# Gate and up weights loaded four neighbouring rows to a partition, with the contraction in that order

## The chip, the cores and the metric

The kernel runs on one core of one Trainium2 chip. The metric is the device time of one execution in microseconds (us). The profiler took one further execution; all rows below are from that one.

## The reference

Two layers. In each, the residual stream `h` (1024 tokens by 1024 features, fp32) goes through an attention mixer and then through a mixture of experts:

```python
def hierarchical_moe(xn, w_group, w_router, w_gate, w_up, w_down):
    ...                       # router: 8 groups x 4 experts, the best group, two experts of it
    def expert_block(args):
        xb, e = args          # rows of one expert
        h = jax.nn.silu(xb @ w_gate[e]) * (xb @ w_up[e])
        return h @ w_down[e]
    ...                       # rows back to their tokens, weighted by the gates, summed
for l in range(DEPTH):
    h = h + hybrid_mixer(rms_norm(h, attn_norm[l]), ...)
    h = h + hierarchical_moe(rms_norm(h, ffn_norm[l]), ...)
return rms_norm(h, final_norm)
```

`w_gate` and `w_up` are [2, 32, 1024, 256] and `w_down` is [2, 32, 256, 1024], all fp32. So one expert has 1 MB each of gate, up and down weights, and one layer's 32 experts have 96 MB, each byte of it read once. A row of a gate or up matrix is 256 floats, 1 KB; a row of a down matrix is 4 KB.

## The kernel before

Every matmul of weights is done in three passes. A weight tile is split by ScalarE into a rounded part `hi` (L1468) and by VectorE into the rest `lo` (L1469), and the helper `mm3` (L195 to L197) multiplies high by high, high by low and low by high.

The experts are taken one after the other, each as one block of at most 96 rows. Per expert the stages are: a gather of its normed rows from DRAM (`xn_d`, written by `norm` in the router stage) by GpSimd's indirect DMA; eight transposes that put the features on the partitions (`flip_x`, L1479), split again into two parts (L185, L186); `gate_up`, 24 matmuls of 512 columns in which chunk k of the contraction multiplies features of chunk k with the gate and up columns of those features side by side; `silu` (L1493 on ScalarE, L1494); two transposes; `down`, 12 matmuls; and a scatter of the results by indirect DMA (L1517). Six pieces of 128 by 1024 weights are split per expert: four of gate and up, two of down. The order of the instructions of TensorE, ScalarE, VectorE and GpSimd is the order of the code; stages of neighbouring experts are interleaved there by hand.

SyncE's queue issues the weight loads. `load_gu` (L350, L351) loads an expert's gate and up weights in two halves `q`, four transfers of 512 KB; `load_dn` (L332) the down weights, one transfer of 1 MB. Gate and up tiles have room for the experts 0 to 4 before the first expert starts. From then on the loads of expert n + 5 are issued in the code where expert n begins, and each waits in SyncE's queue for its tile to come free. A partition of a half holds four rows that lie 128 rows apart in DRAM:

```python
ks = slice(q * 512, q * 512 + 512)
sp.dma_start(raw[q][:, :, 0:FF], wg_[ks].rearrange("(k p) n -> p k n", p=P))
sp.dma_start(raw[q][:, :, FF:], wu_[ks].rearrange("(k p) n -> p k n", p=P))
```

Ahead of the experts, the router stage works through eight tiles of 128 tokens: output projection, residual, `norm`, router. `norm` writes the normed tile with VectorE (L1103) and stores it (L1107). The last tile is done in two halves by GpSimd (`norm_half`, L1125). Expert 0's weights are split there too, with the `lo` parts on GpSimd (`halves`, L1113). The first gather (L1461) waits for the list of rows, at the end of a chain of small VectorE operations.

Of the kernel before, what the change touches and what calls it, by code (L numbers as in the profile page):

```python
# [82 lines left out]
def kernel(ctx: ExitStack, tc: tile.TileContext, x, positions, attn_norm, w_in, b_f, q_norm, w_uq,  # L83
# [48 lines left out]
    # gains, one feature per partition  # L132
# [31 lines left out]
    def rsqrt(dst, v, n, tag, c=1.0):  # L164
        """dst = c * v ** -0.5, with a Newton step behind the engine's own power."""
        y = small.tile([P, n], F32, name="rs_y", tag=f"rs_y{tag}")
        pool.tensor_tensor(y, v, mhalf[:, 0:n], op=OP.pow)  # L167
        t = small.tile([P, n], F32, name="rs_t", tag=f"rs_t{tag}")
        pool.tensor_tensor(t, y, y, op=OP.mult)  # L169
        pool.tensor_tensor(t, t, v, op=OP.mult)  # L170
        pool.tensor_scalar(t, t, -0.5 * c, 1.5 * c, op0=OP.mult, op1=OP.add)  # L171
        pool.tensor_tensor(dst, y, t, op=OP.mult)  # L172
# [9 lines left out]
    def split(hi, lo, src, scale=None):  # L182
        """hi + lo = src * scale, each with as many bits as one pass of the tensor engine carries."""
        if scale is None:
            act.activation(hi, src, AF.Copy)  # L185
            dve.tensor_tensor(lo, src, hi.bitcast(F32), op=OP.subtract)  # L186
        else:
            act.activation(hi, src, AF.Copy, scale=scale)
            dve.scalar_tensor_tensor(lo, src, scale, hi.bitcast(F32), op0=OP.mult, op1=OP.subtract)

    def mm3(ps, sh, sl, mh, ml, kcs, first=True, last=True):
        """ps += s.T @ m over the chunks, three passes."""
        n = len(kcs)
        for i, kc in enumerate(kcs):
            pe.matmul(ps, sh(kc), mh(kc), start=first and i == 0, stop=False)  # L195
            pe.matmul(ps, sh(kc), ml(kc), start=False, stop=False)  # L196
            pe.matmul(ps, sl(kc), mh(kc), start=False, stop=last and i == n - 1)  # L197
# [15 lines left out]
    # DRAM kept between phases  # L213
# [5 lines left out]
    def combined(l, i, ht, y_):  # L219
        """The residual stream's tile behind layer l - 1."""  # L220
        if l == 0:
            return ht
        for j in range(2):
            y = y_(j)
            sp.dma_start(y, y_d[l - 1][j * T + i * P:j * T + (i + 1) * P])
            dve.scalar_tensor_tensor(ht, y, gates[:, j, i:i + 1], ht, op0=OP.mult, op1=OP.add)  # L226
        if l < DEPTH:
            sp.dma_start(h_d[2 * l - 1][i], ht)
        return ht
# [106 lines left out]
    def gu_tiles(p, tags=("mix", "mix"), more=None):  # L336
        r = []
        for t in tags:
            q = p
            if t == "mix":  # L340
                gu_n[0] += 1
                if GUX and gu_n[0] > 8 and gu_n[0] % 9 == 0 and more is not None:
                    q, t = more, "gux"
            r.append(q.tile([P, 4, 2 * FF], F32, name="gu", tag=t))
        return r

    def load_gu(raw, wg_, wu_):
        for q in range(2):
            ks = slice(q * 512, q * 512 + 512)
            sp.dma_start(raw[q][:, :, 0:FF], wg_[ks].rearrange("(k p) n -> p k n", p=P))  # L350
            sp.dma_start(raw[q][:, :, FF:], wu_[ks].rearrange("(k p) n -> p k n", p=P))  # L351
# [6 lines left out]
    def mixer_open(l):  # L358
        """What a layer can load before the one in front of it is through."""
        # room of the latents, which takes tiles of the residual stream first  # L360
# [17 lines left out]
    def mixer(l, opened):  # L378
        h_in = [xv[i] for i in range(NT)] if l == 0 else h_d[2 * l - 1]
        h_out = h_d[2 * l]  # L380
        # operands of a forgetting head as rows: q_hi twice, q_lo, 1, 1, c_hi, c_lo; k_lo, k_hi, -c_hi, -c_lo, 1, 1
# [123 lines left out]
        # ---- values, queries and keys of the forgetting heads; beside it what hangs on misc -  # L505
# [32 lines left out]
        def forget_a():  # L538
            # log_sigmoid(z) = min(z, 0) - log1p(exp(-|z|)); log1p by its series in u / (2 + u)
            z, u, s1, s2 = t_("fz"), t_("fu"), t_("fs"), t_("fs2")  # L540
            fl.update(z=z, u=u, s1=s1, s2=s2)
            dve.tensor_tensor(z, misc[:, :, 0:H], bft[:, l][:, None, :].to_broadcast([P, NT, H]), op=OP.add)
            dve.scalar_tensor_tensor(u, z, -1.0, z, op0=OP.mult, op1=OP.min)
            act.activation(u, u, AF.Exp)
# [17 lines left out]
        def forget_c():  # L562
            # sums within a token tile, and behind them those of the tiles before
# [82 lines left out]
        def v_scale(g, tp):  # L646
            # a power of two that puts the largest value between 2**14 and 2**15
# [28 lines left out]
        def late_pools():  # L676
            # where the values and misc were: weights of the latent projections, tables of the rotation
# [256 lines left out]
        def fin_a(h):  # L934
            # normed rows: y / sqrt(mean(y * y) + eps * Z * Z), with y and Z scaled alike
# [24 lines left out]
        def fin_c(p, half, bank=1):  # L960
            ysb = pairs[p][0].rearrange("p t s d -> p t (s d)")
            # the bank of the second head's results, which the next pair comes to use later
# [10 lines left out]
        # the output projection's weights, two blocks of rows to a piece, where attention has done  # L973
# [120 lines left out]

        def norm(i):
            ht = hts[i]
            sp.dma_start(h_out[i], ht)
            if i < NT - 1:
# [4 lines left out]
                dve.scalar_tensor_tensor(xn, ht, rs[:, i:i + 1], gb, op0=OP.mult, op1=OP.mult)  # L1103
# [5 lines left out]
        def halves(j):  # L1109
            hi, lo = hl[j]  # L1110
            raw = early[0][j // 2][:, j % 2 * 2:j % 2 * 2 + 2].rearrange("p k n -> p (k n)")
            act.activation(hi, raw, AF.Copy)
            pool.tensor_tensor(lo, raw, hi.bitcast(F32), op=OP.subtract)  # L1113
# [3 lines left out]
        def norm_half(c):  # L1117
            """What the last tile's norm can do half by half."""
# [6 lines left out]
            pool.tensor_tensor(xn[:, cs], hts[NT - 1][:, cs], gb[:, cs], op=OP.mult)  # L1125
# [4 lines left out]
        # the router's operands are the tile before its norm: w_rt carries the gains, the gates' exponents the scales  # L1130
# [18 lines left out]
        def route_group(rg, a, b, lg=None):  # L1149
            """Experts, gates and ranks of the tokens of tiles a to b, and their entries in the blocks."""  # L1150
# [43 lines left out]
            # ranks within an expert by token; block NT holds the counts  # L1194
# [23 lines left out]
            # gates  # L1218
# [17 lines left out]
        # weights of the first experts, where attention's values and then its results have been  # L1236
        gu_n[0] = 0
        raw0 = v1.tile([P, 2, 4, 2 * FF], F32, name="V", tag="V")
# [11 lines left out]
        for i in range(NT):  # L1250
# [25 lines left out]
            if i == NT - 1:  # L1276
                # the first expert's gate and up weights in two parts, where those of w_o have been
# [35 lines left out]
        # rows of the blocks: which assignment sits where  # L1313
# [10 lines left out]
        # the experts' counts, and the number of further blocks they need  # L1324
# [7 lines left out]
        # behind the rows of the first experts  # L1332
# [13 lines left out]
    def more_tables(l):  # L1346
        """Blocks for the rows of an expert beyond the first RB: their experts, and which assignment sits where."""
# [28 lines left out]
        # of an assignment: the first further block of its expert, the block and the row its rank puts it in  # L1376
# [11 lines left out]
        # block of + qd - 1 where qd > 0, none elsewhere  # L1388
# [20 lines left out]
    def moe_open(l, v0, v1, mp, early, downs, dn_close, hl, hl_close, spare_close):  # L1409
# [16 lines left out]
        def expert(pools, wg_, wu_, wd_, gi, si, n=None):  # L1426
            """The stages of one block of rows, each to be issued where its engines have time."""
# [6 lines left out]
            def load_a():  # L1434
# [5 lines left out]
                e["raw"] = [raw[q][:, k:k + 2] for q in range(2) for k in (0, 2)]  # L1440
# [24 lines left out]
            def piece(j, eng=dve):  # L1465
                hi, lo = hl.popleft()
                raw = (e["raw"][j] if j < 4 else e["rawd"][j - 4]).rearrange("p k n -> p (k n)")
                act.activation(hi, raw, AF.Copy)  # L1468
                eng.tensor_tensor(lo, raw, hi.bitcast(F32), op=OP.subtract)  # L1469
                e["h"].append(hi)  # L1470
                e["l"].append(lo)
# [10 lines left out]
            def gate_up(q):  # L1482
                if q == 0:
                    e["gu"] = ps_([RB, 2 * FF], F32, name="gu")
                at = lambda w: lambda k: w[k // 2][:, (k % 2) * 512:(k % 2) * 512 + 512]
# [55 lines left out]
    def moe(l, m):  # L1541
# [16 lines left out]
        for n in range(NE + 1):  # L1558
# [19 lines left out]
            if l == DEPTH - 1 and n >= KEPT and len(kept) < NT:  # L1578
                # the weights are through: their room takes the residual stream for the last step
                for raw in gu_tiles(mp):  # L1580
                    for t in range(2):
                        kept.append(raw.rearrange("p k n -> p (k n)")[:, t * D:(t + 1) * D])
# [106 lines left out]
```

## Time and profile before

| What | Value |
|---|---|
| three runs | 1996.01, 1997.6 and 2002.56 us, median 1997.6 |
| profiled execution, first to last instruction | 1997.8 us |
| TensorE busy (matmul) | 1760.9 us, 88% |
| VectorE busy | 1347.5 us, 67% |
| ScalarE busy | 1187.7 us, 59% |
| GpSimd busy | 568.4 us, 28% |
| DMA | 427.11 MB, mean 214 GB/s |

No time of the profiled execution other than its span is given; the span lies 0.2 us over the median of the runs. The shares are means over stages that are limited by different things: attention, the router stage (about 490 to 634 us in layer 0 and 1466 to 1606 us in layer 1), the experts (about 634 to 966 us and 1606 to 1941 us) and the final norm. The expert stage has to be read by itself.

### The profile page before, as it was taken

How to read it: one execution, taken by the hardware profiler on the slowest of the kernel's cores; microseconds unless marked ns; L12 is line 12 of the kernel's file. 1: busy time of each engine (PE TensorE's matmuls, PEld its weight loads, DVE VectorE, ACT ScalarE, POOL GpSimd, SP SyncE). 2: the span in 40 equal slices, each digit the busy share in tenths (PEclk: the TensorE clock that was granted, in tenths of full speed). 3: DMA queues.
4: the chain of work that ended last, by engine and by line, in shares of the span. 5: the costliest groups of instructions: out<-in, count | busy, mean ns of one | idle time of the engine just before them, and what ended most of it. 6: DMA issues, size and time to landing. Idle time of an engine off the chain costs nothing. (4 is left out here: it accounts for less than half of the span.)

```text
span 1997.8 us, 33752 instructions
## 1 busy us (share of the span) xinstructions
PE 1760.9 (88%) x12509; PEld 1420.1 (71%) x12509; DVE 1347.5 (67%) x2172; ACT 1187.7 (59%) x2254; POOL 568.4 (28%) x857
## 2 busy tenths in 40 slices
PE   7999899999995999998499997999999689998870
PEld 6987688888883666666399786888888556666650
DVE  6454388887246888877555355888852678887756
ACT  4443278788214888877344235888841278887751
POOL 4001044234114333331230021623330333332305
PEclk9999999999997999999799998999999889999995
DMA  4257833553755999999742775334455499999986
GB/s 157 64 126 218 261 119 108 114 123 96 251 185 180 345 333 333 327 325 331 284 137 54 203 242 183 126 101 109 114 196 209 148 297 324 327 332 322 321 295 235
DMA packets 243684, 427.11 MB, mean 214 GB/s; under 512 B 22166, under 2 KB 168636, under 8 KB 240444
## 3 DMA queue, kind: packets, MB, share of 16 engines
q1 hardware_dynamic: 228092, 387.14, 61.2%
q0 software_dynamic: 14336, 33.58, 5.2%
q10 hardware_dynamic: 1088, 4.19, 0.7%
q8 instruction: 100, 1.64, 0.3%
q14 instruction: 68, 0.56, 0.1%
HBM read 347.24 MB, written 94.37 MB: 221 GB/s over the span
## 5 line engine op out<-in xcount | busy, mean ns | idle before, releaser
L1469 DVE TENSOR_TENSOR lo<-gu,hi 128x1024 fp32r<-128x1024 f32 x248 | 292.6, 1222 | 41.6 <-ACT hi L1468 41.6
L1468 ACT ACTIVATE hi<-gu 128x1024 fp32r<-128x1024 f32 x248 | 248.4, 1054 | 26.4 <-DMA gu<-in_w_up_dram 20.5
L195 PE MATMUL gu<-hi,V 128*96 128x512 f32 x512 | 214.8, 420 | 38.4 <-ACT V L185 38.4
L885 PE MATMUL S<-op 96*128 96x512 f32 (+3 forms) x960 | 228.8, 372 | 20.2 <-DMA op<-FK 13.2
L897 DVE TENSOR_REDUCE nm<-S 128x1 f32<-128x1024 f32 (+7 forms) x256 | 183.2, 752 | 69.3 <-PE S L889 69.3
L906 ACT ACTIVATE pr<-S,nm 128x1024 f32<-128x1024 f32 (+7 forms) x256 | 188.9, 754 | 38.0 <-DVE nm L897 37.9
L197 PE MATMUL gu<-hi,V 128*96 128x512 f32 x512 | 210.0, 410 | 0.0
L196 PE MATMUL gu<-lo,V 128*96 128x512 f32 x512 | 205.7, 402 | 0.0
L916 ACT ACTIVATE ph<-pt 128x512 f16<-128x512 f32 x288 | 157.1, 600 | 66.8 <-PE pt L914 65.8
L917 DVE SCALAR_TENSOR_TENSOR pl<-pt,ph 128x512 f16<-128x512 f32 x288 | 184.7, 682 | 8.6 <-ACT ph L916 7.8
L885 PEld LDWEIGHTS S<-op 96*128 96x128 f32 (+1 forms) x960 | 161.5, 196 | 37.5 <-DMA wor<-in_w_o_dram 14.5
L1517 POOL DMA_INDIRECT y<-V,sidx x64 | 59.7, 932 | 441.6 <-ACT V L1516 417.4
L914 PE MATMUL pt<-ident,pr 128*128 128x128 f32 x1152 | 154.9, 278 | 8.5 <-ACT pr L906 4.8
L1469 DVE TENSOR_TENSOR lo<-dn,hi 128x1024 fp32r<-128x1024 f32 x128 | 155.9, 1219 | 4.2 <-ACT hi L1468 3.9
L1468 ACT ACTIVATE hi<-dn 128x1024 fp32r<-128x1024 f32 x128 | 134.9, 1055 | 4.7 <-DMA dn<-in_w_down_dram 4.7
L195 PEld LDWEIGHTS gu<-hi,V 128*96 128x96 f32 x512 | 84.9, 166 | 74.1 <-ACT V L185 50.3
L914 PEld LDWEIGHTS pt<-ident,pr 128*128 128x128 f32 x1152 | 125.0, 143 | 13.7 <-ACT pr L906 12.9
L928 PE MATMUL y<-V,ph 128*128 128x64 f16 x2304 | 121.7, 193 | 2.8 <-ACT ph L916 1.6
L197 PEld LDWEIGHTS gu<-hi,V 128*96 128x96 f32 x512 | 84.6, 165 | 53.8 <-DVE V L186 21.9
L928 PEld LDWEIGHTS <-ph 128*128 128x128 f16 x2304 | 116.9, 98 | 5.2 <-ACT ph L916 1.8
L928 PE MATMUL y<-V,pl 128*128 128x64 f16 x1152 | 117.1, 193 | 1.1 <-DVE pl L917 1.0
L186 DVE TENSOR_TENSOR V<-pt,V 128x384 fp32r<-128x384 f32 x128 | 65.5, 552 | 69.1 <-ACT V L185 68.9
(363 smaller groups left out, 4318.5 us busy)
## 6 DMA issues: line engine op xcount, KB each, us to landing
gu<-in_w_gate_dram SPq DMA_DIRECT2D x124, 512.0 KB
gu<-in_w_up_dram SPq DMA_DIRECT2D x124, 512.0 KB
dn<-in_w_down_dram SPq DMA_DIRECT2D x60, 1024.0 KB
raw<-in_w_in_dram SPq DMA_DIRECT2D x48, 256.0 KB
h<-ht SPq DMA_DIRECT2D x17, 512.0 KB
FQ<-st SPq DMA_DIRECT2D x32, 256.0 KB
FK<-st SPq DMA_DIRECT2D x32, 256.0 KB
MQ<-st SPq DMA_DIRECT2D x16, 512.0 KB
```

Source lines behind the costliest of these rows:

```text
L195: pe.matmul(ps, sh(kc), mh(kc), start=first and i == 0, stop=False)
L196: pe.matmul(ps, sh(kc), ml(kc), start=False, stop=False)
L197: pe.matmul(ps, sl(kc), mh(kc), start=False, stop=last and i == n - 1)
L885: pe.matmul(o, a[0:k, qs], b[0:k, c0:c0 + n], start=bank not in started, stop=pi == len(passes) - 1 and not diag, skip_group_check=True)
L897: dve.tensor_reduce(nm, u["S"][:, col:col + (qb + 1) * P], axis=AX.X, op=OP.max, negate=True)
L906: act.activation(u["pr"][:, s], u["S"][:, s], AF.Exp, bias=nm, accum_out=zst[h // 2][:, qb, h % 2:h % 2 + 1])
L914: pe.transpose(pt[:, b], u["pr"][:, (4 * q + b) * P:(4 * q + b + 1) * P], ident)
L916: act.activation(u["ph"][:, ks], pt, AF.Copy, scale=P_SCALE)
L917: dve.scalar_tensor_tensor(u["pl"][:, ks], pt, P_SCALE, u["ph"][:, ks], op0=OP.mult, op1=OP.subtract)
L928: pe.matmul(yst[h][:, qb], a[:, b], v[:, kb, h % H, c], start=first_y[h], stop=(kb == qb and s == 2), skip_group_check=True)
L1468: act.activation(hi, raw, AF.Copy)
L1469: eng.tensor_tensor(lo, raw, hi.bitcast(F32), op=OP.subtract)
```

## The change

The rows of a gate or up matrix are spread over the partitions in another order. Partition p holds rows 8p to 8p + 7, rows 8p to 8p + 3 in half 0 and the other four in half 1, so that what a partition gets in one transfer is one run of 4 KB in DRAM where it was four runs of 1 KB. Gate and up lie in two separate blocks of a tile, where they lay side by side row by row.

Chunk k of the contraction now has the features 8p + k on its partitions. `norm` and `norm_half` write the normed rows with their columns in that order (column 128k + p holds feature 8p + k), so that the gather and the transposes stay as they were. To do so they read the residual tile and the gain eight floats apart. A matmul of `gate_up` reads its 512 moving columns as two runs of 256, and the pieces are split as two runs of 512. No instruction is added, removed or moved on any engine; only access patterns change.

```diff
@@ gu_tiles, load_gu
-            r.append(q.tile([P, 4, 2 * FF], F32, name="gu", tag=t))
+            r.append(q.tile([P, 2, 4, FF], F32, name="gu", tag=t))
...
-            ks = slice(q * 512, q * 512 + 512)
-            sp.dma_start(raw[q][:, :, 0:FF], wg_[ks].rearrange("(k p) n -> p k n", p=P))
-            sp.dma_start(raw[q][:, :, FF:], wu_[ks].rearrange("(k p) n -> p k n", p=P))
+            ks = slice(q * 4, q * 4 + 4)
+            sp.dma_start(raw[q][:, 0], wg_.rearrange("(p k) n -> p k n", k=KC)[:, ks])
+            sp.dma_start(raw[q][:, 1], wu_.rearrange("(p k) n -> p k n", k=KC)[:, ks])
@@ router stage
+        def by_chunk(t):
+            return t.rearrange("r (p k) -> r k p", k=KC)
+
+        def chunked(t):
+            return t.rearrange("r (k p) -> r k p", k=KC)
...
-                dve.scalar_tensor_tensor(xn, ht, rs[:, i:i + 1], gb, op0=OP.mult, op1=OP.mult)
+                dve.scalar_tensor_tensor(chunked(xn), by_chunk(ht), rs[:, i:i + 1], by_chunk(gb), op0=OP.mult, op1=OP.mult)
@@ halves
-            raw = early[0][j // 2][:, j % 2 * 2:j % 2 * 2 + 2].rearrange("p k n -> p (k n)")
+            raw = early[0][j // 2][:, :, j % 2 * 2:j % 2 * 2 + 2].rearrange("p g k n -> p g (k n)")
+            hi, lo = (w.rearrange("p (g n) -> p g n", g=2) for w in (hi, lo))
@@ norm_half
-            pool.tensor_tensor(xn[:, cs], hts[NT - 1][:, cs], gb[:, cs], op=OP.mult)
+            ps_ = slice(c * P // 2, c * P // 2 + P // 2)
+            pool.tensor_tensor(chunked(xn)[:, :, ps_], by_chunk(hts[NT - 1])[:, :, ps_], by_chunk(gb)[:, :, ps_], op=OP.mult)
@@ expert: load_a, piece, gate_up
-                e["raw"] = [raw[q][:, k:k + 2] for q in range(2) for k in (0, 2)]
+                e["raw"] = [raw[q][:, :, k:k + 2].rearrange("p g k n -> p g (k n)") for q in range(2) for k in (0, 2)]
...
-                raw = (e["raw"][j] if j < 4 else e["rawd"][j - 4]).rearrange("p k n -> p (k n)")
-                act.activation(hi, raw, AF.Copy)
-                eng.tensor_tensor(lo, raw, hi.bitcast(F32), op=OP.subtract)
+                raw = e["raw"][j] if j < 4 else e["rawd"][j - 4].rearrange("p k (g n) -> p (k g) n", g=2)
+                h_, l_ = (w.rearrange("p (g n) -> p g n", g=2) for w in (hi, lo))
+                act.activation(h_, raw, AF.Copy)
+                eng.tensor_tensor(l_, raw, h_.bitcast(F32), op=OP.subtract)
...
-                at = lambda w: lambda k: w[k // 2][:, (k % 2) * 512:(k % 2) * 512 + 512]
+                at = lambda w: lambda k: w[k // 2].rearrange("p (g k n) -> p g k n", g=2, k=2)[:, :, k % 2]
```

## Rows read from the trace of the kernel before

**Rows 1.** The page's part 2: the span in 40 equal slices, DMA share in tenths, GB/s

```profile
DMA  4257833553755999999742775334455499999986
GB/s 157 64 126 218 261 119 108 114 123 96 251 185 180 345 333 333 327 325 331 284 137 54 203 242 183 126 101 109 114 196 209 148 297 324 327 332 322 321 295 235
```

**Rows 2.** Busy us by stretch: stretch, length, five engines (x instructions), PEclk, DMA share, GB/s

```profile
740.00:850.00 110.00, 105.63 (x516) 73.13 (x515) 94.36 (x112) 91.24 (x134) 35.83 (x33) 1.00 1.02 329
867.00:956.00 89.00, 79.65 (x371) 54.66 (x370) 68.83 (x80) 64.90 (x96) 18.77 (x18) 0.96 1.02 333
1820.00:1930.00 110.00, 98.14 (x458) 67.53 (x457) 85.09 (x100) 80.53 (x117) 26.06 (x24) 0.95 1.02 335
```

**Rows 3.** Timeline of ScalarE: the silu of experts 2, 22, 31, then of 21, 31

```profile
658.90 0.36 ACT L1493 ACTIVATE hs<-gu 96x256 f32<-96x256 f32 x1
...
857.23 0.36 ACT L1493 ACTIVATE hs<-gu 96x256 f32<-96x256 f32 x1
...
955.63 0.38 ACT L1493 ACTIVATE hs<-gu 96x256 f32<-96x256 f32 x1 [1.51 <-PE gu L197]
...
1819.55 0.36 ACT L1493 ACTIVATE hs<-gu 96x256 f32<-96x256 f32 x1
...
1930.19 0.38 ACT L1493 ACTIVATE hs<-gu 96x256 f32<-96x256 f32 x1 [1.51 <-PE gu L197]
```

**Rows 4.** Waits, 860 to 956 us, then 1820 to 1930 us: total us, times, longest

```profile
PEld gu L195 <- ACT V L185: 11.4, 9, 3.6
ACT hi L1468 <- DMA gu<-in_w_up_dram: 10.0, 7, 3.6
...
ACT hi L1468 <- DMA gu<-in_w_up_dram: 10.4, 6, 4.0
```

**Rows 5.** Timeline of SyncE's queue: first gate load of experts 5 and 31, each layer

```profile
640.32 0.37 SPq L350 DMA_DIRECT2D gu<-in_w_gate_dram  x1
...
930.59 0.73 SPq L350 DMA_DIRECT2D gu<-in_w_gate_dram  x1
...
1612.05 0.37 SPq L350 DMA_DIRECT2D gu<-in_w_gate_dram  x1
...
1906.13 1.15 SPq L350 DMA_DIRECT2D gu<-in_w_gate_dram  x1
```

**Rows 6.** DMA view, 526 to 529 us (gate, up loads), then 1946 to 1949 us

```profile
DMA packets 1079, 1.07 MB, mean 357 GB/s; under 512 B 32, under 2 KB 1079, under 8 KB 1079
...
DMA packets 343, 1.24 MB, mean 412 GB/s; under 512 B 41, under 2 KB 41, under 8 KB 343
```

**Rows 7.** Two lines by themselves: duration in ns min/median/max, and the forms

```profile
L1178 DVE TENSOR_REDUCE ing<-tmp x6: 261/271/380, 562.8 to 1587.5; 128x8 f32<-128x64 f32 x4, 128x16 f32<-128x128 f32 x2
...
L1203 DVE TENSOR_REDUCE ee<-tmp x6: 286/286/421, 576.2 to 1592.2; 128x4 f32<-128x128 f32 x4, 128x8 f32<-128x256 f32 x2
```

**Rows 8.** Timeline of layer 0's last token tile, VectorE and GpSimd: start, us, what

```profile
595.87 1.28 DVE L1103 SCALAR_TENSOR_TENSOR xn<-ht,rs,gb 128x1024 f32<-128x1024 f32 x1
...
599.99 1.26 POOL L1125 TENSOR_TENSOR xn<-ht,gb 128x512 f32<-128x512 f32 x1 [5.75 <-DMA xn<-xn]
603.69 2.37 POOL L1113 TENSOR_TENSOR lo<-V,hi 128x1024 fp32r<-128x1024 f32 x1 [2.44 <-ACT hi L1112]
606.01 1.33 POOL L1125 TENSOR_TENSOR xn<-ht,gb 128x512 f32<-128x512 f32 x1
...
609.84 6.95 POOL L1113 TENSOR_TENSOR lo<-V,hi 128x1024 fp32r<-128x1024 f32 x3
...
610.01 2.21 DVE L1168 TENSOR_TENSOR eg<-eg,kg 128x16 f32<-128x16 f32 x1
...
616.85 0.17 DVE L1165 TENSOR_TENSOR e<-e,revg 128x8 f32<-128x8 f32 x1
...
624.33 1.26 POOL L1461 DMA_INDIRECT V<-xn,gidx  x1 [6.54 <-DVE gd L1221]
```

**Rows 9.** Matmuls by shape, 500 to 625 us, then the page's part 5

```profile
L1197 PE MATMUL rt<-OHs,onesb 128*128 128x256 bf16 x1 | 0.3, 270 | 0.0
...
L1197 PE MATMUL rt<-OHs,onesb 128*128 128x64 bf16 x1 | 0.2, 217 | 0.0
...
L195 PE MATMUL gu<-hi,V 128*96 128x512 f32 x512 | 214.8, 420 | 38.4 <-ACT V L185 38.4
```

More of the change, by code (lines that the diff above doesn't have):

```diff
@@ L1237, in mixer @@
         gu_n[0] = 0
-        raw0 = v1.tile([P, 2, 4, 2 * FF], F32, name="V", tag="V")
+        raw0 = v1.tile([P, 2, 2, 4, FF], F32, name="V", tag="V")
         early = [[raw0[:, 0], raw0[:, 1]]]
@@ L1581, in moe @@
                     for t in range(2):
-                        kept.append(raw.rearrange("p k n -> p (k n)")[:, t * D:(t + 1) * D])
+                        kept.append(raw[:, t].rearrange("p k n -> p (k n)"))
                         sp.dma_start(kept[-1], h_d[2 * l][len(kept) - 1])
```

## The prediction

> **What bounds the kernel now.** The change touches the expert stages and the norm in front of them, so I read those by themselves. I began with the slices of the page. The DMA share is at nine tenths in twelve of 40 slices, in two stretches, and these are the two expert stages [rows 1]. Full engines alone don't say that anyone waits for them, so the next view is the busy time by stretch [rows 2]. From 740 to 850 us TensorE's matmuls fill 105.63 of 110 us (0.96) at full granted clock, although the DMA share is 1.02 there. From 867 to 956 us they fill 79.65 of 89 (0.89), and from 1820 to 1930 us 98.14 of 110 (0.89), with the DMA engines as full as before. So TensorE sets the pace for most of a stage and something else does towards its end.
>
> The third view gives the size. There is one silu for each expert, and its start shows the rhythm [rows 3]. From expert 2 to expert 22 of layer 0 it is 857.23 - 658.90 = 198.33 us for 20 experts, 9.92 us each: TensorE's own pace. From expert 22 to expert 31 it is 98.40 us for 9 experts, where 89.25 would do: 9.15 us lost. In layer 1, expert 21 to expert 31 takes 1930.19 - 1819.55 = 110.64 us for 10 experts, against 99.17: 11.47 us lost. Together **20.6 us**, which is the most that faster weights can give back at this pace.
>
> The view of waits names the cause. In the late stretches ScalarE stands before the split of a gate and up piece until the load has landed, 10.0 us in layer 0 and 10.4 us in layer 1 [rows 4]. What TensorE's own row shows there, 11.4 us until ScalarE's split of the transposed rows, is the same delay one step on: that split stands in ScalarE's queue behind the piece that waits.
>
> Last, why late in the stage. Expert 5's first gate load is issued at 640.32 us and expert 31's at 930.59 us [rows 5]: 26 experts in 290.27 us, 11.16 us each, against TensorE's 9.92. The store of experts loaded ahead is used up by 1.2 us an expert until it is empty. Layer 1: 1906.13 - 1612.05 = 294.08 us, 11.31 us each.
>
> **The change part by part.**
>
> *The loads.* An expert's gate and up weights are 2.097 MB. Now they come as 2048 packets of 1 KB, afterwards as 512 of 4 KB. The trace has stretches with one size alone [rows 6]. With 1 KB packets, 1079 of them in 3 us, the engines move 357 GB/s; with 4 KB packets, 343 less the 41 small ones, 412 GB/s, both with the engines full. So the same bytes take 2.097 MB / 357 GB/s = 5.87 us now and 2.097 / 412 = 5.09 us then: 0.78 us less for each expert. Both stretches are undisturbed; in the expert stage the mean is 329 GB/s [rows 2], so everything takes longer there and the difference hardly less. Bounds: nothing below, if the engines give the expert stage some 330 GB/s whatever the packets are, and 0.78 x 357 / 329 = 0.85 us above. I take 0.78.
>
> How much is needed? To lose nothing, expert 31's loads would have to come 9.15 us earlier in layer 0 and 11.47 us in layer 1. Spread over 26 experts that is 0.35 us an expert (11.16 to 10.81) and 0.44 (11.31 to 10.87). 0.78 is well above both, so the store isn't empty before the end, TensorE keeps 9.92 us to the last expert and the gain is the whole 20.6 us. What lies above 0.44 buys nothing: with the loads at about 10.4 to 10.5 us, TensorE is the bound throughout.
>
> [...]
>
> *The loads at other places.* Five experts' weights come during the router stage, in the shadow of TensorE's projection. They get shorter by the same 0.78 us each and nobody waits for them in a row that I found; nothing.
>
> *The pieces and their matmuls.* The splits on ScalarE and VectorE read two runs of 512 where they read one of 1024. They have cover: in 110 us VectorE is busy 94.36 and ScalarE 91.24 [rows 2], so the 11 experts' 66 pieces could each cost 0.23 us more before VectorE is full. I take nothing. The 24 matmuls of an expert's gate_up have no such cover; there are 3 x 512 = 1536 in both layers [rows 9]. For a moving operand in several runs the nearest row is the count of ranks, L1197, which repeats runs of 32 columns: 217 ns for 2 runs and 270 ns for 8, and 192 more columns lie in that difference too. If the columns cost nothing, a run would cost at most 53 / 6 = 9 ns; if they account for it, nothing. I take nothing and keep 1536 x 9 ns = 13.6 us as the upper end.
>
> *The norm.* Its reads step eight floats. The nearest row is a reduction with a step of four floats, L1178: 261 ns for 64 elements, 380 for 128, 1.86 ns an element; a contiguous one, L1203, has 286 ns for 128 and 421 for 256, 1.05 ns [rows 7]. So a stepped element costs about 0.8 ns more. On VectorE's normed tile of 1024 that is 0.8 us, seven times a layer. These are hidden: of the last of them only the store matters, because GpSimd's first half of the last tile waits for it [rows 8]. That half starts at 599.99, takes 1.26 us, and GpSimd's next operation waits for ScalarE until 603.69 anyway; 2.4 us of cover.
>
> GpSimd's second half, at 606.01, is bare. Behind it in its queue stand the scale of the last tile and three subtractions (6.95 us from 609.84), and while these run VectorE's two-input operations stall (2.21 us for one of 128x16 elements, where one of 128x8 takes 0.17 behind them) [rows 8]. VectorE goes on freely at 616.85, and its chain ends in the first gather at 624.33, on which expert 0 waits. So a longer second half can shift the expert stage by as much. Price: 512 x 0.8 ns = 0.4 us a layer by VectorE's rows; bounds 0 (VectorE's chain gets ahead while GpSimd is late, and catches up) and a doubling, 1.33 us. I take 0.4 us, 0.8 us in both layers.
>
> [...]
>
> *Sum.* Against the profiled span of 1997.8 us: 1997.8 - 20.6 + 0.8 = **1978.0 us**. The span is 0.2 us above the median of the runs, 1997.6; I let that stand.
>
> **The rivals.**
>
> *Only a part comes back.* Loads gain less under contention than in the undisturbed stretches, or the indirect gathers and scatters, which share the engines, take some of it. For it: 329 GB/s in the stage against 357 with 1 KB packets alone, so packets aren't all that slows the loads. Against: the need is little more than half of 0.78. At half of the need, 0.2 us an expert, about half the loss stays: 1988 us.
>
> *No gain.* The stage is limited by what memory gives, not by packets, and the loads keep 11.2 us an expert. For it: the rate is between 321 and 345 GB/s in eleven of the twelve full slices [rows 1]. Against: stretches in rows 6 reach 412. The price is that of the norm alone: 1997.8 + 0.8 = 1998.6 us. [...]
>
> *Slower: the two runs cost TensorE time.* Every gate_up matmul pays a pause at the jump between the gate and the up run. TensorE is the bound for 20 of 32 experts already, so all of it would count, and slower experts need their loads later, so the 20.6 us come back anyway. It decides from (20.6 - 0.8) / 1536 = 13 ns a matmul; at 25 ns it is 38.4 us: 1978.0 + 38.4 = 2016 us. Against: at most 9 ns by rows 9.
>
> **How the numbers follow.** Whole gain 0.70, with its own range 1974 to 1983 us (the norm between 0 and 2.7 us, some of the loss left, a little more gained where the last experts run quicker than 9.92). A part, 1983 to 1991: 0.12. No gain, within 0.3% of 1997.6: 0.10. Slower: 0.08. A change within 0.3%, 6 us, can hardly be told from none here, as the runs before spread by 6.5 us. Faster by more than 0.3% (below 1991.6) is then 0.82, the same 0.10, slower 0.08. The range 1973 to 1990 us holds the whole gain and most of the second case.
>
> **What would show it.** Right: silus 9.92 us apart up to expert 31 in both layers; ScalarE's wait for gate and up loads near nothing in the late stretches; expert 31's first gate load some 10 us earlier after expert 5's; a DMA share that falls below 1 or a rate above 340 GB/s; L1103's successor near 2.1 us and L1125's near 1.7 us. Wrong: the same late gaps with 4 KB packets at 330 GB/s (second or third case), or gaps of over 10 us between silus from expert 2 on with TensorE's matmuls longer (fourth).

## The result

The changed kernel takes **1978.0 us** (median of 4 runs, 1977.16 to 1979.87) against 1996.8 us of the kernel before on the same chip (4 runs). The ratio is 0.9897, 95% interval 0.9878 to 0.9917: faster by about 1%, beyond the 0.3% within which the forecast could not tell a change from none. The profiled execution's span is 1978.1 us, against 1997.8. The device time of the changed kernel's profiled execution is 1979.87 us, 1.8 us above its span, and a device time lies as far above its span in the other kernels' runs. For the profiled execution of the kernel before only the span is on record, so its 1997.8 us is not to be compared with the medians directly.

The first view is the page's part 2 of the changed kernel, the answer to [rows 1].

```profile
DMA  4257732553754999998742775344456479999966
GB/s 158 65 130 218 258 125 100 113 128 79 274 181 156 335 367 366 360 353 307 246 141 54 205 239 189 125 104 108 108 186 226 156 259 358 362 360 357 345 217 219
```

The stretches of full DMA engines are still there, but they move some 360 GB/s where it was some 330, and they end earlier.

The busy time by stretch (columns as in [rows 2]) tells whether TensorE is held up at the end of a stage.

```profile
740.00:850.00 110.00, 105.61 (x515) 73.03 (x514) 94.25 (x112) 91.29 (x134) 35.82 (x33) 1.00 1.00 361
867.00:940.00 73.00, 69.85 (x342) 48.24 (x340) 62.13 (x73) 59.62 (x90) 18.26 (x18) 1.00 0.92 319
1800.00:1905.00 105.00, 100.61 (x489) 69.34 (x488) 89.57 (x107) 86.50 (x128) 28.84 (x27) 1.00 0.96 338
```

TensorE's share is now 0.96 in the late stretches too (69.85 of 73, 100.61 of 105), where it was 0.89, and its granted clock there is 1.00, where it was 0.96 and 0.95. The DMA share has fallen to 0.92 and 0.96 there, from 1.02: the loads are through before the stage is (in layer 0 the last transfer of expert 31's weights is issued at 914.63 us, and its silu comes at 946.19). The first stretch has the same busy times on VectorE and ScalarE as before (94.25 and 91.29 us, against 94.36 and 91.24), so splitting a piece as two runs costs neither of them anything that shows.

The rhythm, by the same silus as in [rows 3]: experts 2, 22 and 31 of layer 0, then 21 and 31 of layer 1.

```profile
658.81 0.36 ACT L1504 ACTIVATE hs<-gu 96x256 f32<-96x256 f32 x1
...
857.19 0.36 ACT L1504 ACTIVATE hs<-gu 96x256 f32<-96x256 f32 x1
...
946.19 0.38 ACT L1504 ACTIVATE hs<-gu 96x256 f32<-96x256 f32 x1 [1.51 <-PE gu L197]
...
1809.69 0.37 ACT L1504 ACTIVATE hs<-gu 96x256 f32<-96x256 f32 x1
...
1908.62 0.38 ACT L1504 ACTIVATE hs<-gu 96x256 f32<-96x256 f32 x1 [1.51 <-PE gu L197]
```

Experts 22 to 31 take 89.00 us where they took 98.40, and 21 to 31 of layer 1 take 98.93 where they took 110.64: 9.4 and 11.7 us, 21.1 us together. The waits from 860 to 956 us hold no row of ScalarE waiting for a gate or up load any more. What is left of the answer to [rows 4] is 0.58 us an expert for the transposed rows, as in the stretch from 740 to 850 us, where there is no wait for a gate or up load either (6.4 us for 11 experts):

```profile
PEld gu L195 <- ACT V L185: 5.2, 9, 0.6
```

SyncE's queue, first gate load of experts 5 and 31 of each layer, answers to [rows 5].

```profile
641.00 0.33 SPq L351 DMA_DIRECT2D gu<-in_w_gate_dram  x1
...
905.57 0.33 SPq L351 DMA_DIRECT2D gu<-in_w_gate_dram  x1
...
1603.13 0.34 SPq L351 DMA_DIRECT2D gu<-in_w_gate_dram  x1
...
1869.56 0.33 SPq L351 DMA_DIRECT2D gu<-in_w_gate_dram  x1
```

From expert 5 to expert 31 it is 264.6 us in layer 0 and 266.4 in layer 1, 25.7 and 27.7 us less than before, where the forecast looked for some 10. Only 9.4 and 11.7 of it come out of the stage; the rest is margin.

The norm of layer 0, answering to [rows 8]: the lines of VectorE and GpSimd by themselves (duration in ns min/median/max), then GpSimd's second half, its three subtractions, VectorE's first operation that is slow beside them (2.23 us, where the shortest of that line takes 0.17), and the first gather.

```profile
L1111 DVE SCALAR_TENSOR_TENSOR xn<-ht,rs,gb x14: 2081/2396/2418, 513.7 to 1558.8; 128x1024 f32<-128x1024 f32 x14
...
L1135 POOL TENSOR_TENSOR xn<-ht,gb x4: 2046/2068/2094, 601.4 to 1569.0; 128x512 f32<-128x512 f32 x4
```

```profile
606.37 2.09 POOL L1135 TENSOR_TENSOR xn<-ht,gb 128x512 f32<-128x512 f32 x1
...
610.89 6.95 POOL L1122 TENSOR_TENSOR lo<-V,hi 128x1024 fp32r<-128x1024 f32 x3
611.06 2.23 DVE L1178 TENSOR_TENSOR eg<-eg,kg 128x16 f32<-128x16 f32 x1
...
625.40 1.26 POOL L1471 DMA_INDIRECT V<-xn,gidx  x1 [6.54 <-DVE gd L1231]
```

Both operations are slower than before by more than was forecast, and the chain shifts as described: the three subtractions start 1.05 us later, and the first gather 1.07 us later. Not all of that is the norm's. The start of the scale of the last tile but one (L176 on GpSimd), which lies ahead of the last tile's halves, already comes 0.35 us later than before, and counted from it the gather is 0.72 us late. The first silu of the layer isn't late at all. Before, then changed:

```profile
592.31 0.19 POOL L176 TENSOR_SCALAR rs_v<-ss 128x1 f32<-128x1 f32 x1 [13.06 <-ACT xn L1101]
...
641.70 0.38 ACT L1493 ACTIVATE hs<-gu 96x256 f32<-96x256 f32 x1 [1.94 <-PE gu L197]
```

```profile
592.66 0.19 POOL L176 TENSOR_SCALAR rs_v<-ss 128x1 f32<-128x1 f32 x1 [14.62 <-ACT xn L1109]
...
641.61 0.38 ACT L1504 ACTIVATE hs<-gu 96x256 f32<-96x256 f32 x1 [1.15 <-PE gu L197]
```

The ledger of the two profiled spans: up to expert 31's silu of layer 0, 955.63 - 946.19 = 9.4 us gained; from there to expert 31's silu of layer 1, 974.6 - 962.4 = 12.1 us; from there to the end, 67.6 against 69.5, 1.9 us lost. The sum is 19.7 us before rounding (9.44 + 12.13 - 1.87), which is the difference of the spans.

### The profile page after: what moved, and what is told of

The parts are those of the page before. It is cut to its first block, busy times and chain, and to the rows that moved or that the text cites. A ratio compares the mean times of both kernels' runs of the same rounds, so it can differ in the third digit from the quotient of the medians.

```text
span 1978.1 us, 33744 instructions
## 1 busy us (share of the span) xinstructions
PE 1754.6 (89%) x12509; PEld 1414.8 (72%) x12509; DVE 1361.8 (69%) x2172; ACT 1188.2 (60%) x2254; POOL 568.7 (29%) x857
## 5 line engine op out<-in xcount | busy, mean ns | idle before, releaser
L1480 DVE TENSOR_TENSOR lo<-gu,hi 128x1024 fp32r<-128x1024 f32 x248 | 292.5, 1221 | 18.8 <-ACT hi L1479 18.8
L1479 ACT ACTIVATE hi<-gu 128x1024 fp32r<-128x1024 f32 x248 | 248.2, 1054 | 0.0
L195 PE MATMUL gu<-hi,V 128*96 128x512 f32 x512 | 210.9, 412 | 24.4 <-ACT V L185 24.4
L197 PE MATMUL gu<-hi,V 128*96 128x512 f32 x512 | 207.0, 404 | 0.0
```

What stands on the lines that cost most here:

```text
L1479: act.activation(h_, raw, AF.Copy)
L1480: eng.tensor_tensor(l_, raw, h_.bitcast(F32), op=OP.subtract)
```

## The experiments

All kernels ran beside the kernel before. In the first group of four its median was 1997.8 us (17 runs), in the second group of three 1997.5 us (23 runs).

**The size of the packets by itself.** All of the change's tiles, splits and two-run matmuls stay, but the partitions hold the old rows 128 apart, and the norm writes in the old order.

```diff
-            sp.dma_start(raw[q][:, 0], wg_.rearrange("(p k) n -> p k n", k=KC)[:, ks])
-            sp.dma_start(raw[q][:, 1], wu_.rearrange("(p k) n -> p k n", k=KC)[:, ks])
+            sp.dma_start(raw[q][:, 0], wg_.rearrange("(k p) n -> p k n", p=P)[:, ks])
+            sp.dma_start(raw[q][:, 1], wu_.rearrange("(k p) n -> p k n", p=P)[:, ks])
...
-                dve.scalar_tensor_tensor(chunked(xn), by_chunk(ht), rs[:, i:i + 1], by_chunk(gb), op0=OP.mult, op1=OP.mult)
+                dve.scalar_tensor_tensor(xn, ht, rs[:, i:i + 1], gb, op0=OP.mult, op1=OP.mult)
...
```

> The change's tiles, splits and matmuls (two blocks, two runs), with the rows of before: four runs of 1 KB, 128 rows apart, and the norm of before; the output is the reference's. If the packet's size is what gave the time: no gain, 1995 to 1999 us, silus late from expert 22 on, packets of 1 KB at about 330 GB/s in the expert stage. If it was the tile's layout (each transfer fills one run of 4 KB of a partition): 1978 us. If the two-run matmuls cost 9 ns each they show here as up to 13 us on top.

Measured: 1998.5 us (12 runs), ratio 1.0001, interval 0.9986 to 1.0017. The whole gain is gone. Its profiled execution was the longest of the twelve (span 2009.3 us), but the picture in it is that of the kernel before; here the late stretches, with TensorE at 63.77 of 73 (0.87) and 94.59 of 110 (0.86):

```profile
867.00:940.00 73.00, 63.77 (x291) 43.61 (x290) 55.55 (x65) 51.89 (x76) 16.47 (x16) 0.95 1.02 321
...
1820.00:1930.00 110.00, 94.59 (x426) 64.34 (x425) 80.37 (x94) 77.09 (x113) 24.09 (x23) 0.94 1.02 322
```

So the gain is in what one packet holds, not in the tiles' layout. Whether it is fewer packets or longer runs of neighbouring bytes in DRAM that helps, no kernel of the study separates. And as this kernel keeps the two-run matmuls and is no slower than before (1998.5 us against 1997.8), these cost nothing that can be measured: the rival that rested on them is out.

**Packets of half the size.** Two neighbouring rows to a partition, packets of 2 KB, and the norm in the order that belongs to them (a step of two floats). The eight transposes of an expert take their chunks in the sequence that goes with it.

```diff
-            sp.dma_start(raw[q][:, 0], wg_.rearrange("(p k) n -> p k n", k=KC)[:, ks])
-            sp.dma_start(raw[q][:, 1], wu_.rearrange("(p k) n -> p k n", k=KC)[:, ks])
+            rows = lambda w: w[q * 512:q * 512 + 512].rearrange("(a p t) n -> p a t n", a=2, t=2)
+            sp.dma_start(raw[q][:, 0].rearrange("p (a t) n -> p a t n", t=2), rows(wg_))
+            sp.dma_start(raw[q][:, 1].rearrange("p (a t) n -> p a t n", t=2), rows(wu_))
...
-            return t.rearrange("r (p k) -> r k p", k=KC)
+            return t.rearrange("r (j t) -> r t j", t=2)
...
-                        k = 4 * q + c
+                        k = c % 2 * 4 + 2 * q + c // 2
```

> Two neighbouring rows to a partition and run, 2 KB packets; the norm steps two floats in place of eight; the output is the reference's. From the packet cost that the two sizes of the prediction imply (5.87 us for 1 KB, 5.09 for 4 KB, the same overhead for each packet), 2 KB should take about 5.35 us, 0.52 us less an expert, over the 0.35 and 0.44 that are needed: the whole gain, 1976 to 1979 us, no late silu in layer 0 and at most a trace of one in layer 1. If the gain goes with the load time instead, two thirds of it: 1984 us.

Measured: 1977.3 us (6 runs), ratio 0.9893, interval 0.9873 to 0.9914. The whole gain again. The DMA view of 740 to 850 us, where the engines are full, for the changed kernel, then for 2 KB and for 1 KB (the kernel of the experiment above):

```profile
DMA packets 11580, 39.72 MB, mean 361 GB/s; under 512 B 1900, under 2 KB 1900, under 8 KB 11572
```

```profile
DMA packets 16612, 38.75 MB, mean 352 GB/s; under 512 B 1877, under 2 KB 1877, under 8 KB 16604
```

```profile
DMA packets 25145, 36.02 MB, mean 327 GB/s; under 512 B 1790, under 2 KB 21229, under 8 KB 25137
```

The rate rises with the packet: 327, 352, 361 GB/s. These are rates of everything in the stretch; the down weights come in 4 KB rows in all three kernels. The time does not follow the rate. At 2 KB the loads of experts 5 to 31 take 10.49 us each in layer 0 and 10.53 in layer 1 (273.7 us for 26), below the 10.81 and 10.87 that the forecast called the need, and nothing is lost. With both packets the store of experts lasts to the end, and the faster loads of 4 KB bought nothing more (1978.0 us, against 1977.3 with 2 KB); the other outcome that was written down, 1984 us in proportion to the load time, is out. At which pace between those of 1 KB and 2 KB packets the loss ends, no run shows.

**Each side's own pace.** To see what the loads do when TensorE doesn't hold them up, the third pass of gate_up is left out (8 of 24 matmuls an expert), once in the changed kernel and once in the kernel before.

```diff
-            pe.matmul(ps, sh(kc), ml(kc), start=False, stop=False)
-            pe.matmul(ps, sl(kc), mh(kc), start=False, stop=last and i == n - 1)
+            pe.matmul(ps, sh(kc), ml(kc), start=False, stop=not low and last and i == n - 1)
+            if low:
+                pe.matmul(ps, sl(kc), mh(kc), start=False, stop=last and i == n - 1)
...
-                    range(4 * q, 4 * q + 4), first=q == 0, last=q == 1)
+                    range(4 * q, 4 * q + 4), first=q == 0, last=q == 1, low=False)
```

> The changed kernel without the third pass of gate_up (16 of 24 matmuls an expert; the low part of the rows is left out), so that TensorE needs about 8.2 us an expert and the loads bound the late part of the stage: it shows the loads' own pace with 4 KB packets. Theory by the period measured in the changed kernel (a load is issued every 10.2 us with full engines): late silus 10.1 to 10.3 us apart. By the forecast's 0.78 us: 10.4 to 10.5 us. Rival (the period there was held up by TensorE, the loads could do much better): 9.6 us or less. The time about 1940 to 1965 us.

> The same cut in the kernel before: the third pass of gate_up left out, 1 KB packets. Theory (the loads bound it): late silus 11.2 to 11.3 us apart, from an earlier expert on than in the kernel before, and the end of a layer's experts hardly earlier, 0 to 4 us a layer: 1989 to 1998 us. The difference to the same cut with 4 KB packets prices the packets with TensorE out of the way: 0.78 us for each expert over 26 experts and two layers would be 41 us, 1.0 us would be 52 us. Rival (TensorE's pace set it, packets don't matter): both cuts take the same time, 70 us or more below the kernel before.

Measured: 1962.2 us with 4 KB packets (4 runs, 1957.0 to 1964.8), ratio 0.9819 to the kernel before, interval 0.9794 to 0.9844. With 1 KB packets 2002.1 us (10 runs, 1993.3 to 2009.0), ratio 1.0023, interval 1.0008 to 1.0038. The silus of experts 12 and 29 of layer 0, then of layer 1, first with 4 KB:

```profile
747.09 0.36 ACT L1505 ACTIVATE hs<-gu 96x256 f32<-96x256 f32 x1
922.03 0.36 ACT L1505 ACTIVATE hs<-gu 96x256 f32<-96x256 f32 x1
...
1698.97 0.36 ACT L1505 ACTIVATE hs<-gu 96x256 f32<-96x256 f32 x1
...
1875.19 0.37 ACT L1505 ACTIVATE hs<-gu 96x256 f32<-96x256 f32 x1
```

And with 1 KB:

```profile
747.86 0.36 ACT L1494 ACTIVATE hs<-gu 96x256 f32<-96x256 f32 x1
...
937.64 0.37 ACT L1494 ACTIVATE hs<-gu 96x256 f32<-96x256 f32 x1
...
1715.87 0.37 ACT L1494 ACTIVATE hs<-gu 96x256 f32<-96x256 f32 x1
...
1905.89 0.36 ACT L1494 ACTIVATE hs<-gu 96x256 f32<-96x256 f32 x1
```

Seventeen experts take 174.94 and 176.22 us with 4 KB, 10.29 and 10.37 us each; with 1 KB 189.78 and 190.02 us, 11.16 and 11.18 each. These are the loads' own paces: in the early part, where loads are still ahead, the silus of both kernels are 8.7 us apart, and here ScalarE waits for the down weights, which are loaded through the same queue. The waits from 740 to 850 us, with 4 KB, then with 1 KB:

```profile
ACT hi L1480 <- DMA dn<-in_w_down_dram: 17.4, 10, 2.2
```

```profile
ACT hi L1469 <- DMA dn<-in_w_down_dram: 21.4, 10, 2.7
```

TensorE's 9.92 us with all three passes lies under both paces. The difference is 0.81 to 0.87 us an expert. From the first silu to the last of each layer the same two executions differ by 19.3 and 20.1 us, 0.76 us over 2 x 26 experts, and the medians differ by 39.9 us, 0.77. The profiled execution with 1 KB is the fastest of its ten, 8.8 us under their median, so the true difference may be somewhat larger.

The pair also says which engine bounds each kernel. The same third of gate_up's matmuls is worth some 16 us where packets are 4 KB (1978.0 to 1962.2, from two groups of runs) and nothing where they are 1 KB (2002.1 us, against 1997.5). With 1 KB the kernel even came out 4.7 us slower than the kernel before, outside the 1989 to 1998 us that were expected; why is open.

**The norm put back in order.** The changed kernel with the norm of the kernel before.

```diff
-                dve.scalar_tensor_tensor(chunked(xn), by_chunk(ht), rs[:, i:i + 1], by_chunk(gb), op0=OP.mult, op1=OP.mult)
+                dve.scalar_tensor_tensor(xn, ht, rs[:, i:i + 1], gb, op0=OP.mult, op1=OP.mult)
...
-            pool.tensor_tensor(chunked(xn)[:, :, ps_], by_chunk(hts[NT - 1])[:, :, ps_], by_chunk(gb)[:, :, ps_], op=OP.mult)
+            pool.tensor_tensor(xn[:, cs], hts[NT - 1][:, cs], gb[:, cs], op=OP.mult)
```

> The change without its stepped norm reads: the normed rows are stored in feature order, so the experts multiply the wrong features (the output is wrong in that part, the work is the same). In the trace of the changed kernel the first gather of layer 0 starts 1.07 us later than before (625.40 against 624.33), yet the silu of expert 0 doesn't (641.61 against 641.70). If the norm's price is on the path, 1.0 us a layer comes back: some 1976 us. If it is absorbed between the gather and the first matmuls: 1978 us, and the silu of expert 0 is again within 0.2 us of where it was.

Measured: 1977.2 us (6 runs), ratio 0.9891, interval 0.9870 to 0.9911; 0.8 us under the changed kernel, less than the intervals can tell apart. The first silu of layer 0 is neither within 0.2 us of where it was nor 1 us earlier: it comes 2.4 us earlier than in the changed kernel, at 639.18 us. That isn't this norm's price, for L176 of the last tile but one is 2.7 us earlier already, and the kernel with the step in the transposes, its norm in order too, has its first silu at 641.63 us:

```profile
589.95 0.19 POOL L176 TENSOR_SCALAR rs_v<-ss 128x1 f32<-128x1 f32 x1 [13.07 <-ACT xn L1109]
...
639.18 0.38 ACT L1504 ACTIVATE hs<-gu 96x256 f32<-96x256 f32 x1 [1.92 <-PE gu L197]
```

So this run decides nothing on a price of 1 us.

**The norm by itself.** The opposite cut: the kernel before with the stepped norm alone, edited at the same two places in the other direction.

```diff
-                dve.scalar_tensor_tensor(xn, ht, rs[:, i:i + 1], gb, op0=OP.mult, op1=OP.mult)
+                dve.scalar_tensor_tensor(chunked(xn), by_chunk(ht), rs[:, i:i + 1], by_chunk(gb), op0=OP.mult, op1=OP.mult)
...
```

> The kernel before with the change's norm alone: the normed rows are stored with their columns in the new order, the weights and the contraction are left in the old one, so that normed features and weights don't belong together. Theory (the norm costs little and is absorbed): VectorE's normed tile about 2.40 us and GpSimd's half about 2.07 us, as in the changed kernel, against 1.28 and 1.30; the first gather of a layer 0 to 1.1 us later; the time 1997.8 + 0 to 2 us, no difference that can be measured. Rival (the gain of the whole change hides a real price of the norm, which late weights or the rise of the clock pay back in the changed kernel): the first silu of a layer comes 1 us or more later in both layers and the time is 2 to 4 us over the kernel before.

Measured: 1997.4 us (12 runs), ratio 0.9999, interval 0.9984 to 1.0014. The two lines have the prices that they have in the changed kernel, here with the mean of one in ns behind the busy us:

```profile
L1109 DVE SCALAR_TENSOR_TENSOR xn<-ht,rs,gb 128x1024 f32<-128x1024 f32 x14 | 32.8, 2345 | 26.1 <-POOL rs L172 22.8 <-DMA ht<-in_x_dram 3.2
L1132 POOL TENSOR_TENSOR xn<-ht,gb 128x512 f32<-128x512 f32 x4 | 8.3, 2071 | 13.8 <-DMA xn<-xn 13.8
```

The first silus come at 641.26 and 1613.20 us, against 641.70 and 1613.89 before, so they aren't late. So 1 us more on each of 14 tiles and 0.8 us more on each of four halves don't reach the time by anything that the intervals show, neither with late weights behind them nor without. The interval is about 3 us wide to either side, so a price of 1 us in the sum is neither shown nor excluded.

**The step in the transposes.** The norm writes in the old order, as above, and the eight transposes of an expert read their rows eight floats apart instead.

```diff
-                        pe.transpose(pt[:, c], e["x"][:, k * P:(k + 1) * P], ident[0:RB, 0:RB])
+                        pe.transpose(pt[:, c], e["x"].rearrange("r (p k) -> r k p", k=KC)[:, k], ident[0:RB, 0:RB])
```

> 4 KB rows as in the change, but the normed rows are stored in feature order and the transposes of an expert's rows read every eighth column (512 transposes of 96 by 128 in both layers); the output is the reference's. If TensorE reads stepped columns at no price, it is the time of the run without the stepped norm, 1976 to 1978 us. If a stepped read costs it what VectorE pays (1.1 us for 1024 elements, so about 1 ns a column), 100 ns a transpose on the engine that is the bound: 51 us more, about 2028 us.

Measured: 1977.2 us (6 runs), ratio 0.9892, interval 0.9872 to 0.9912. A transpose got longer by a tenth, as the mean ns of one shows, first in the changed kernel, then with the step:

```profile
L1490 PE MATMUL pt<-ident,V 96*128 96x96 f32 x352 | 37.6, 251 | 19.4 <-DMA V<-xn,gidx 19.4
```

```profile
L1490 PE MATMUL pt<-ident,V 96*128 96x96 f32 x352 | 46.0, 275 | 19.2 <-DMA V<-xn,gidx 19.2
```

That is no more time for the stage: the silus stay 9.92 us apart. With the norm stepped, in order, or its work moved to TensorE, the three kernels lie between 1977.2 and 1978.0 us. Neither these nor the kernel with 2 KB packets beat the changed kernel by what can be measured.

## Why the prediction was right

**The bound and the 20.6 us: right to 0.5 us.** The forecast read two losses from the silus, 9.15 and 11.47 us. Between the same experts 9.4 and 11.7 came back. The rest is the last expert, which runs in 9.61 us rather than the 9.92 that the forecast counted, as it had allowed for. The cause is shown: bring back 1 KB packets, with the norm that belongs to them, and the loss is back (1998.5 us); put the norm back in order alone and nothing changes (1977.2); keep 1 KB packets and take the norm alone and nothing changes (1997.4).

**The loads: right in size, and more than the need bought nothing.** The forecast worked 0.78 us an expert out of two short stretches with one packet size each [rows 6], with bounds of 0 and 0.85. With TensorE out of the way the runs gave 0.77 by the medians and 0.81 to 0.87 between experts 12 and 29 of the profiled executions, at the upper bound and just over it. The loads' pace was put at 10.4 to 10.5 us and is 10.3 to 10.4. One step was loose, though it did no harm: the 11.16 and 11.31 us from expert 5 to expert 31 were taken as the loads' pace, but the first of these loads wait for TensorE at some 9.9 us, so the mean is a mixture. From expert 10 on in layer 0 (690.73 us) and from expert 9 on in layer 1 (1653.35 us) they come 11.42 and 11.49 us apart. Spread over these 21 and 22 experts alone the need would be 0.44 and 0.52 us, still less than 0.78. In the changed kernel the mean from 5 to 31 fell by 0.99 and 1.06 us; it is a mixture too, 10.18 and 10.25 us where the loads' own pace is 10.3 to 10.4, and so no measure of what the packets save.

**Splits and two-run matmuls at nothing: right.** VectorE and ScalarE have the same busy time in the same stretch (a gate and up piece takes ScalarE 1054 ns as before and VectorE 1221 against 1222), and a gate_up matmul takes as long as before, as the page's part 5 of the changed kernel shows against [rows 9]:

```profile
L195 PE MATMUL gu<-hi,V 128*96 128x512 f32 x512 | 210.9, 412 | 24.4 <-ACT V L185 24.4
```

The mean is 412 ns against 420, where up to 9 ns more were held open.

**The norm: both prices too low, and no harm done.** The term "0.8 us on VectorE's normed tile" measured 1.1 us (2.40 against 1.28), and the term "0.4 us on GpSimd's second half" 0.76 us (2.09 against 1.33). The step that failed is the price per element taken from a reduction that steps through one source by four floats; here two sources step by eight, and an element cost 1.1 ns more on VectorE and 1.5 ns more on GpSimd, which had been priced by VectorE's rows.

The mechanism, GpSimd's second half pushing three subtractions and with them VectorE's chain, is in the trace up to the gather. Counted from L176 of the last tile but one, the first gather of layer 0 comes after 32.02 to 32.05 us in the five profiled executions with the norm in order, after 32.20 us with a step of two floats and after 32.72 to 32.74 us in the three with a step of eight. That prices the longer half at 0.70 us on this chain; in layer 1 it is as much. The longer operation on VectorE's tile costs nothing there: the second half starts 13.7 us after L176 in every kernel, as the forecast's cover said.

Behind the gather the delay ends in the kernels with three passes: gather to silu takes 16.2 us where it took 17.4, and from L176 to the first silu of layer 0 it is 48.85 to 49.39 us with the norm in order and 48.95 and 49.00 us with a step of eight. In the pair of kernels without the third pass it doesn't end: there the first silu comes 1.6 us later in layer 0 and 0.7 us later in layer 1 with the step (and 4 KB packets) than without. So that the norm costs no time holds for this kernel and isn't a rule. In TensorE's view of 622 to 642 us the granted clock is 0.63 against 0.60 before; whether that has to do with the shorter way from gather to silu wasn't tried.

**The sum** fell on 1978.0 with two parts outside it that cancel, and that it agrees to the tenth is luck. Up to the last silu 9.4 + 12.1 = 21.5 us came back, where 20.6 less the norm's 0.8 were counted; against this, the end of the program behind that silu took 1.9 us longer than in the profile before (69.5 against 67.6 us). It is 68.4 to 69.4 us in every other kernel of the study, 68.4 and 68.8 in the two that keep the old packets and tiles, so most of it isn't the change's doing; the kernel before was profiled once, and why it is at 67.6 us there is open. The base was loose as well: 1997.8 is a span, and the 1978.0 that was measured is a device time, which lies 1.8 us above its span. By the spans 19.7 us came back and by the medians 18.8, where 19.8 were forecast.

**The rivals.** "No gain" is out, as the late gaps are gone. "Only a part" is out twice, by the changed kernel and by 2 KB packets, which save less and still give all. "Slower" is out by the kernel that keeps the two-run matmuls with 1 KB rows (1998.5 us).

## What to carry to other kernels

Where loads are ahead at first and late at the end, the loss is read from the rhythm of one operation per unit of work, and what a faster load must save is that loss divided by the units over which it builds up; more than that bought nothing here (1977.3 us with 2 KB, 1978.0 with 4 KB). The packet was worth looking at even at 1 KB here, with the DMA engines full (327 GB/s, against 352 with 2 KB and 361 with 4 KB): rows that lie together can go to one partition if the contraction follows their order, and the side that has to be brought into that order should be the one whose engine waits anyway (a choice by reasoning: here the norm and the transposes came out alike, 1978.0 and 1977.2 us). A pace is taken from a stretch in which that engine alone sets it; if there is none, a kernel that leaves out work of the other engine makes one.

## What was not expected of the hardware

- The step had a price that depended on its width. VectorE's scalar_tensor_tensor of 128x1024 takes 1.28 us in order, 1.28 us with a step of two floats on both sources and 2.40 us with a step of eight. GpSimd's tensor_tensor of 128x512 takes 1.30, 1.52 and 2.07 us. The rows of the kernel with 2 KB packets:

```profile
L1111 DVE SCALAR_TENSOR_TENSOR xn<-ht,rs,gb x14: 1277/1285/1289, 513.6 to 1555.8; 128x1024 f32<-128x1024 f32 x14
...
L1135 POOL TENSOR_TENSOR xn<-ht,gb x4: 1489/1522/1559, 600.2 to 1565.9; 128x512 f32<-128x512 f32 x4
```

- With runs of 4 KB a gate load's issue took SyncE's queue 0.33 us in the median, where it took 0.82 with runs of 1 KB. The shortest are 0.33 and 0.37, and with runs of 2 KB the median is 1.01 and the shortest 0.37, so the medians don't follow the size of the runs; what the longer issues wait for was not shown.
- Leaving out a third of gate_up with 1 KB packets made the kernel 4.7 us slower (interval 0.08% to 0.38%) with a wider spread of its runs (15.6 us in ten runs, against 7.8 in four with 4 KB and the same cut). Its mean granted clock is 0.939 to 0.942 in every run, where the kernel before has 0.949 to 0.953 and the same cut with 4 KB 0.948 to 0.954. Why it is slower was not settled.
